# A gated linear unit on one core: three load slots and products in place, for two load slots and two output slots

## The chip, the cores and the metric

The kernel runs on one core of a Trainium2 chip. The metric is the time of one execution on the device in microseconds, taken as the median of several runs. Four engines of the core matter here: ACT (ScalarE) computes the sigmoid and issues the stores, DVE (VectorE) and POOL (GpSimd) multiply, SP (SyncE) issues the loads. The transfers themselves are done by 16 DMA engines that all queues of the core share.

## What is computed

```python
def setup_inputs():
    return {"x": np.random.randn(8192, 8192).astype(np.float32)}

def reference(x):
    a, b = np.split(x, 2, axis=-1)
    return a * (1 / (1 + np.exp(-b)))
```

Of each row of 8192 floats the first half, a, is multiplied by the sigmoid of the second half, b. 268.4 MB are read and 134.2 MB are written, each byte once.

## The kernel before

**Tiles.** The 8192 rows are cut into 32 tiles of 256 rows (line 20). A tile has two rows of x on each of the 128 partitions, so that a partition holds 64 KiB of input (row 0: a, b; row 1: a, b) and 32 KiB of output (line 21 and 22 lay out the two tensors accordingly; both sides of each transfer are contiguous on a partition). The output of a tile is again two rows, one behind the other.

**Slots.** There are two load slots of 64 KiB and two output slots of 32 KiB on each partition (lines 25 and 26). Tile i uses load slot i mod 2 and output slot i mod 2.

**Work on a tile** (`work`, lines 72 to 89). ACT replaces b by its sigmoid in the load slot (line 82). DVE or POOL multiplies a by it and writes the product to the output slot (line 84). A middle tile is worked on in two pieces, each over both rows: the first 768 columns (`cut`, line 30), whose product POOL makes from tile 2 on, and the other 3328, whose product DVE makes. The first and the last tile are worked on in four pieces, half a row each (`fourths`, line 32), by DVE alone.

**Transfers.** A load is one DMA of 8 MB issued by SP (line 63); the first tile's load is two DMAs, one for each row (line 37). A store is one DMA of 4 MB issued by ACT (line 68). The first tile is stored as two DMAs of 16 KiB on a partition, one for each row; the last one as one of 16 KiB and two of 8 KiB (line 39). For the last tile, `behind` is 1 (line 40), so that its first store stands behind the third sigmoid in ACT's order.

**Order and waits.** The waits are chosen by hand: `place` (line 48) declares for each instruction that it depends, within its slot, on nothing but the instructions handed to it, and keeps it in program order on its engine.

- Load i+2 waits for the products of tile i, which are the last readers of its slot (line 62). It does not wait for a store.
- The sigmoids of tile i wait for load i, and in the middle tiles for store i-2, which frees the output slot (lines 78 to 82). In the last tile the products wait for that store (line 88).
- A product waits for its sigmoid, a store for the products that it sends (line 69).

The loop (lines 93 to 103) issues, for each tile, its sigmoids and products, then load i+2 on SP, then the store on ACT. So the sigmoids of tile i+1 stand behind store i on ACT, which itself waits for the products of tile i.

Two functions rework the finished program and are the same before and after: `_launch_early` moves the first load to the front of SP's program, and `_close_on_sync` shortens the end, so that SP waits last for the last store.

Of the kernel before, what the change touches and what calls it, by code (L numbers as in the profile page):

```python
# [8 lines left out]
def _tiles(ctx, tc, x, out):  # L9
    nc = tc.nc  # L10
    P = nc.NUM_PARTITIONS
    DEP = mybir.DependencyInfo(mybir.DependencyClass.Sync, mybir.DependencyReason.DATA)
    fp32 = mybir.dt.float32
    SIG = mybir.ActivationFunctionType.Sigmoid

    n_rows, n_cols = x.shape
    half = n_cols // 2
    R = 2
    SLOTS = 2
    n_tiles = n_rows // (P * R)  # L20
    x_g = x.rearrange("(g p h r) m -> g h p (r m)", p=P, h=2, r=R)
    out_g = out.rearrange("(g p h r) m -> g h p (r m)", p=P, h=2, r=R)

    pool = ctx.enter_context(tc.tile_pool(name="io", bufs=1))
    xs = [pool.tile([P, R * n_cols], fp32, name=f"x_sb{k}") for k in range(SLOTS)]
    os = [pool.tile([P, R * half], fp32, name=f"o_sb{k}") for k in range(SLOTS)]

    whole = [(0, 8)]
    rows = [(0, 4), (4, 8)]
    cut = half // 16 * 3  # L30
    few_and_most = [(0, 8, 0, cut), (0, 8, cut, half)]
    fourths = [(k, k + 2, k % 4 * half // 4, (k % 4 + 2) * half // 4) for k in range(0, 8, 2)]
    loads = [whole] * n_tiles
    works = [few_and_most] * n_tiles
    stores = [whole] * n_tiles
    behind = [0] * n_tiles
    loads[0] = stores[0] = rows
    works[0] = works[-1] = fourths
    stores[-1] = [(0, 4), (4, 6), (6, 8)]
    behind[-1] = 1  # L40

    def meet(a, b):
        return a[0] < b[1] and b[0] < a[1]

    traced = [[] for _ in range(SLOTS)]
    load_of, mul_of, store_of = {}, {}, {}

    def place(i, ins, *needs):


        kept = {n.ins.name for n in needs}
        for e in traced[i % SLOTS]:
            if e.ins.name not in kept:
                tc.declare_no_dep(ins.ins, e.ins, reason="follows from the waits that are kept")
        traced[i % SLOTS].append(ins)
        tc.keep_in_program_order(ins)
        return ins

    def load(i):
        for lo, hi in loads[i]:  # L60
            c = slice(lo * n_cols // 4, hi * n_cols // 4)
            free = [m for w, m in mul_of.get(i - SLOTS, []) if meet(w, (lo, hi))]
            ins = nc.sync.dma_start(out=xs[i % SLOTS][:, c], in_=x_g[i // 2, i % 2, :, c])  # L63
            load_of.setdefault(i, []).append(((lo, hi), place(i, ins, *free)))

    def store(i, lo, hi):
        c = slice(lo * half // 4, hi * half // 4)
        ins = nc.scalar.dma_start(out=out_g[i // 2, i % 2, :, c], in_=os[i % SLOTS][:, c])  # L68
        done = [m for w, m in mul_of[i] if meet(w, (lo, hi))]
        store_of.setdefault(i, []).append(((lo, hi), place(i, ins, *done)))  # L70

    def work(i, lo, hi, near, far):

        rows = xs[i % SLOTS].rearrange("p (r h m) -> p r h m", r=R, h=2)
        packed = os[i % SLOTS].rearrange("p (r m) -> p r m", r=R)
        r, c = slice(lo // 4, (hi + 3) // 4), slice(near, far)
        b = rows[:, r, 1, c]
        landed = [s for w, s in load_of[i] if meet(w, (lo, hi))]
        gone = [s for w, s in store_of.get(i - SLOTS, []) if meet(w, (lo, hi))]
        by_sigmoid = 0 < i < n_tiles - 1  # L80
        needs = [*landed, *(gone if by_sigmoid else ())]
        sig = place(i, nc.scalar.activation(out=b, in_=b, func=SIG), *needs)  # L82
        engine = nc.gpsimd if far == cut and i > 1 else nc.vector
        mul = engine.tensor_mul(out=packed[:, r, c], in0=rows[:, r, 0, c], in1=b)  # L84
        if by_sigmoid:
            for s in gone:
                tc.add_manual_dep(sig.ins, s.ins.name, DEP, reason="frees the output slot")
        place(i, mul, sig, *(() if by_sigmoid else gone))
        mul_of.setdefault(i, []).append(((lo, hi), mul))

    for i in range(SLOTS):
        load(i)
    for i in range(n_tiles):
        due = list(stores[i])
        for k, piece in enumerate(works[i]):
            work(i, *piece)
            ready = works[i][k - behind[i]][1] if k >= behind[i] else 0
            while len(stores[i]) > 1 and k < len(works[i]) - 1 and due[0][1] <= ready:
                store(i, *due.pop(0))
        if i + SLOTS < n_tiles:  # L100
            load(i + SLOTS)
        for lo, hi in due:
            store(i, lo, hi)


def _launch_early(nc):
# [68 lines left out]
@with_exitstack  # L175
def kernel(
    ctx: ExitStack,
    tc: tile.TileContext,
    x: bass.AP,
    out: bass.AP,  # L180
):
    nc = tc.nc
    with ExitStack() as pools:
        _tiles(pools, tc, x, out)
    tc.close()
    tc.compile()
    _launch_early(nc)
    _close_on_sync(nc)
# [30 lines left out]
```

## Time and profile before

| | us |
|---|---|
| median of 3 runs (932.70 to 932.84) | 932.84 |
| the profiled execution, first to last instruction | 931.1 |
| ACT busy | 229.8 |
| DVE busy | 232.5 |
| POOL busy | 99.9 |
| a middle tile's sigmoids (two pieces) | 1.48 and 5.73 |
| its products (POOL, DVE) | 3.44 and 7.09 |
| a sigmoid of half a row, a product of half a row | 1.90, 2.29 |
| a 4 MB store, from issue to landing (median) | 43.6 |
| an 8 MB load, from issue to landing (median) | 43.5 |

The profiled execution has no total time beside its span. The medians of the runs lie 1.7 us above the span; they hold what lies around it.

How to read it: "q1" is the DMA queue of SP (the loads), "q10" that of ACT (the stores). A time from issue to landing holds the time that a transfer stands behind others, and the time in which it shares the DMA engines with the other queue. "ACTq" and "SPq" are the sequencers of ACT and SP, which issue DMAs and wait. A line of the timeline has the start, the time from the start of the first to the end of the last of the instructions merged in it, engine, operation and shape, and in brackets how long the engine stood idle before, and what ended that.

### The profile page before, as it was taken

Reading aid. Unit: us, or ns where it says so; the run is one execution under the profiler, and the core shown is the slowest. Engines: PE = TensorE matmul, PEld = TensorE weight load, DVE = VectorE, ACT = ScalarE, POOL = GpSimd, SP = SyncE. Lnnn points to the kernel's source line nnn. Section 1 sums busy time; section 2 is a strip of 40 time slices with the busy share of each in tenths; the row PEclk is TensorE's granted clock in tenths of the full one; section 3 lists DMA queues with packets and bytes.
Section 4 is the critical chain, followed back from the end, with each engine's and each line's share of the span. In section 5 each row is a group of like instructions: output and inputs, shape, how many; then the busy total and the mean of one; then the engine's idle time right before and its main releaser. Section 6 shows DMA issues by size and latency. Waiting matters only on the chain.

```text
span 931.1 us, 325 instructions
## 1 busy us (share of the span) xinstructions
DVE 232.5 (25%) x39; ACT 229.8 (25%) x69; POOL 99.9 (11%) x33
## 2 busy tenths in 40 slices
DVE  1133311333113331133320333203332033320233
ACT  2123332033320333203332023320233302333023
POOL 0001111011110111101111011110111101111010
DMA  9999999999999999999999999999999999999998
GB/s 405 450 439 417 428 450 424 455 405 428 450 428 450 407 469 409 428 450 427 452 405 450 428 428 450 424 452 408 428 450 428 450 408 465 411 428 450 427 452 383
DMA packets 9793, 402.67 MB, mean 432 GB/s; under 512 B 1088, under 2 KB 1088, under 8 KB 1088
## 3 DMA queue, kind: packets, MB, share of 16 engines
q1 hardware_dynamic: 4752, 268.44, 66.6%
q10 hardware_dynamic: 5040, 134.22, 33.4%
q14 instruction: 1, 0.01, 0.0%
HBM read 268.44 MB, written 134.22 MB: 432 GB/s over the span
## 4 chain that ended last, share of the span: by engine, by line
DMA 75%; DVE 12%; ACT 12%; issue 0%; ACTq 0%; SPq 0%
DMA out_dram<-o_sb 65%; DVE o_sb L84 12%; ACT x_sb L82 12%; DMA x_sb<-in_x_dram 10%; ACTq L68 0%; SPq L63 0%
## 5 line engine op out<-in xcount | busy, mean ns | idle before, releaser
L84 DVE TENSOR_TENSOR o_sb<-x_sb 128x6656 f32<-128x6656 f32 (+2 forms) x39 | 232.5, 5970 | 690.2 <-ACT x_sb L82 690.2
L82 ACT ACTIVATE x_sb<-x_sb 128x1536 f32<-128x1536 f32 (+1 forms) x68 | 228.5, 3407 | 689.9 <-DMA out_dram<-o_sb 630.0
L84 POOL TENSOR_TENSOR o_sb<-x_sb 128x1536 f32<-128x1536 f32 x29 | 99.7, 3437 | 787.7 <-ACT x_sb L82 787.7
L82 ACT ACT_TABLE_LOAD x1 | 1.3, 1283 | 0.8 <-PEq L203 0.8
L203 POOL MEMSET const-float32-0.0<- 128x1 f32 x1 | 0.1, 98 | 0.2 <-issue 0.2
L203 POOL MEMSET const-bfloat16-1.0<- 128x1 bf16 x1 | 0.1, 101 | 0.0
L203 POOL MEMSET const-uint8-127<- 128x1 uint8 x1 | 0.1, 101 | 0.0
L203 POOL MEMSET const-float32-1.0<- 128x1 f32 x1 | 0.1, 98 | 0.0
## 6 DMA issues: line engine op xcount, KB each, us to landing
out_dram<-o_sb ACTq DMA_DIRECT2D x30, 4096.0 KB, 43.6
x_sb<-in_x_dram SPq DMA_DIRECT2D x2, 4096.0 KB, 16.4
out_dram<-o_sb ACTq DMA_DIRECT2D x3, 2048.0 KB, 28.0
out_dram<-o_sb ACTq DMA_DIRECT2D x2, 1024.0 KB, 8.3
x_sb<-in_x_dram SPq DMA_DIRECT2D x31, 43.5
```

The source lines that it names most:

```text
L82: sig = place(i, nc.scalar.activation(out=b, in_=b, func=SIG), *needs)
L84: mul = engine.tensor_mul(out=packed[:, r, c], in0=rows[:, r, 0, c], in1=b)
L203: nc = _bacc.Bacc("TRN2", target_bir_lowering=False, num_devices=1)
```

## The change

- Three load slots of 64 KiB, no output slots. Together they take the same 192 KiB of a partition.
- Products overwrite the slot's row 0: the product of row 0 goes where a of row 0 was, the product of row 1 where b of row 0 was (`product`). So the 32 KiB of output lie together at the slot's start and are stored from there.
- Three loads are issued ahead of the loop (the first still as two DMAs). Load i+3 waits for the landing of store i, where load i+2 waited for the products of tile i.
- Sigmoids (`gate`) wait for their load alone.
- In the first and the last tile each product also waits for the products before it in the tile, since row 1's products overwrite what row 0's have read.
- The first tile is stored as 8 KiB (after its first product, with the store ahead of the second sigmoid on ACT) and 24 KiB (after its last), where it was 16 and 16. The last tile is stored as before: 16, 8 and 8 KiB, the first behind the third sigmoid.
- In the loop load i+3 comes behind store i in the program, each on its own engine.

```diff
-    SLOTS = 2
+    SLOTS = 3
...
-    os = [pool.tile([P, R * half], fp32, name=f"o_sb{k}") for k in range(SLOTS)]
...
+    few = half // 16 * 3
+    by_fourths = [(r, h * half // 2, (h + 1) * half // 2) for r in (0, 1) for h in (0, 1)]
...
     def load(i):
-        for lo, hi in loads[i]:
-            c = slice(lo * n_cols // 4, hi * n_cols // 4)
-            free = [m for w, m in mul_of.get(i - SLOTS, []) if meet(w, (lo, hi))]
+        for r in (0, 1) if i == 0 else (None,):
+            c = slice(None) if r is None else slice(r * n_cols, (r + 1) * n_cols)
             ins = nc.sync.dma_start(out=xs[i % SLOTS][:, c], in_=x_g[i // 2, i % 2, :, c])
-            load_of.setdefault(i, []).append(((lo, hi), place(i, ins, *free)))
...
+            load_of.setdefault(i, []).append(place(i, ins, *store_of.get(i - SLOTS, [])))
+
+    def store(i, lo, hi, *done):
+        ins = nc.scalar.dma_start(out=out_g[i // 2, i % 2, :, lo:hi], in_=xs[i % SLOTS][:, lo:hi])
+        store_of.setdefault(i, []).append(place(i, ins, *done))
+
+    def gate(i, rows, c):
+        b = xs[i % SLOTS].rearrange("p (r h m) -> p r h m", r=R, h=2)[:, rows, 1, c]
+        landed = load_of[i] if len(load_of[i]) == 1 else [load_of[i][rows.start]]
+        return place(i, nc.scalar.activation(out=b, in_=b, func=SIG), *landed)
+
+    def product(i, engine, r, c, *needs):
+
+        v = xs[i % SLOTS].rearrange("p (r h m) -> p r h m", r=R, h=2)
+        ins = engine.tensor_mul(out=v[:, 0, r, c], in0=v[:, r, 0, c], in1=v[:, r, 1, c])
+        return place(i, ins, *needs)
+
+    def ends(i, stores):
+        done = []
+        for k, (r, lo, hi) in enumerate(by_fourths):
+            c = slice(lo, hi)
+            done.append(product(i, nc.vector, slice(r, r + 1), c, gate(i, slice(r, r + 1), c), *done))
+            for a, z, after, at in stores:
+                if at == k:
+                    store(i, a, z, *done[: after + 1])
+
+    def middle(i):
+        done = []
+        for engine, c in ((nc.gpsimd if i > 1 else nc.vector, slice(0, few)), (nc.vector, slice(few, half))):
+            sig = gate(i, slice(0, 2), c)
+            done.append(product(i, engine, slice(0, 2), c, sig))
+        store(i, 0, R * half, *done)
+
+    q = half // 2
     for i in range(SLOTS):
         load(i)
     for i in range(n_tiles):
...
+        if i == 0:
+            ends(i, [(0, q, 0, 0), (q, 4 * q, 3, 3)])
+        elif i == n_tiles - 1:
+            ends(i, [(0, 2 * q, 1, 2), (2 * q, 3 * q, 2, 3), (3 * q, 4 * q, 3, 3)])
+        else:
+            middle(i)
         if i + SLOTS < n_tiles:
             load(i + SLOTS)
-        for lo, hi in due:
-            store(i, lo, hi)
```

More of the change, by code (lines that the diff above doesn't have):

```diff
@@ L11, in _tiles @@
     P = nc.NUM_PARTITIONS
-    DEP = mybir.DependencyInfo(mybir.DependencyClass.Sync, mybir.DependencyReason.DATA)
     fp32 = mybir.dt.float32
@@ L25, in _tiles @@
     xs = [pool.tile([P, R * n_cols], fp32, name=f"x_sb{k}") for k in range(SLOTS)]
-    os = [pool.tile([P, R * half], fp32, name=f"o_sb{k}") for k in range(SLOTS)]
[L28 to L43, printed above, removed]
+    few = half // 16 * 3
+    by_fourths = [(r, h * half // 2, (h + 1) * half // 2) for r in (0, 1) for h in (0, 1)]
     traced = [[] for _ in range(SLOTS)]
@@ L59, in load @@
     def load(i):
-        for lo, hi in loads[i]:
-            c = slice(lo * n_cols // 4, hi * n_cols // 4)
-            free = [m for w, m in mul_of.get(i - SLOTS, []) if meet(w, (lo, hi))]
+        for r in (0, 1) if i == 0 else (None,):
+            c = slice(None) if r is None else slice(r * n_cols, (r + 1) * n_cols)
             ins = nc.sync.dma_start(out=xs[i % SLOTS][:, c], in_=x_g[i // 2, i % 2, :, c])
-            load_of.setdefault(i, []).append(((lo, hi), place(i, ins, *free)))
[L66 to L89, printed above, removed]
+            load_of.setdefault(i, []).append(place(i, ins, *store_of.get(i - SLOTS, [])))
@@ L93, in _tiles @@
     for i in range(n_tiles):
[L94 to L99, printed above, removed]
+        if i == 0:
[4 more added lines that the diff above has]
+            middle(i)
         if i + SLOTS < n_tiles:
             load(i + SLOTS)
-        for lo, hi in due:
-            store(i, lo, hi)
 def _launch_early(nc):
```

## The prediction

> **What bounds the kernel now.** I read the page first, then a table of stretches, the two tables of waits (engines, then SP's queue), the timeline at both ends, and last the packet records of the trace, where each DMA engine's descriptors stand with start, length and bytes. The page:
>
> ```profile
> span 931.1 us, 325 instructions
> DMA  9999999999999999999999999999999999999998
> q1 hardware_dynamic: 4752, 268.44, 66.6%
> q10 hardware_dynamic: 5040, 134.22, 33.4%
> HBM read 268.44 MB, written 134.22 MB: 432 GB/s over the span
> ```
>
> No slice of the DMA row is empty, and the two queues' shares add up to 100% of 16 engines. The stretches (columns: stretch, length, DVE, ACT and POOL busy, clock, DMA share, GB/s) say that the rate is the same for loads alone (11 to 21), for the mixture and for stores alone (912 to 920, 438; packets are counted whole, so short stretches swing):
>
> ```profile
> 11.00:21.00 10.00, 4.49 (x2) 3.71 (x2) 0.00 (x0) 1.00 1.01 433
> 46.00:910.00 864.00, 214.53 (x31) 213.67 (x60) 99.67 (x29) 1.00 1.00 433
> 912.00:920.00 8.00, 6.40 (x3) 6.65 (x4) 0.00 (x0) 1.00 1.01 438
> ```
>
> The records agree: a 64 KiB load packet takes 2.418 us, a 32 KiB store packet 1.213, a 16 KiB one 0.611, an 8 KiB one 0.309, in every part of the run. All data packets added up and divided by 16 engines are 930.8 us, of a span of 931.1. Empty are only the first 1.01 us, before the first load packet, and about 0.3 at the end. The waits look worse than they are:
>
> ```profile
> ACT x_sb L82 <- DMA out_dram<-o_sb: 630.0, 29, 22.1
> ```
> ```profile
> SPq L63 <- DVE o_sb L84: 855.5, 30, 32.1
> ```
>
> ACT waits 630 us for stores and SP 855 us for products, but the transfers behind those waits are in a line that never runs dry. The chain of waits agrees: 75% of the span is DMA, and the 12% each of ACT and DVE on it are periods in which the engines moved other tiles.
>
> So the kernel is bound by bytes through 16 engines. The change moves the same bytes, in the same 264 load packets and 280 store packets for each engine (the packet counts above, less 16 completion records for each of 33 and 35 DMAs, over 16). It can gain under 1 us. It can lose wherever both queues are empty at once.
>
> **The order of packets.** In the records load and store packets alternate one to one on each engine once both queues hold work, whatever their size: a round is 2.42 + 1.21 = 3.63 us, a tile 8 rounds, 29.0 us. Call the lead the number of load packets that start before the first store packet. It is 17 now (the first store packet starts at 23.58, after the first packet of tile 1's load). When the last load packet ends, 264 - 17 = 247 store packets are done; tile 30's store ends with packet 256, so 9 are left, 10.9 us. The records: loads end at 910.10, that store at 921.00. This backlog is what covers the last tile's computing:
>
> ```profile
> 911.66 5.51 ACT L82 ACTIVATE x_sb<-x_sb 128x2048 f32<-128x2048 f32 x3 [21.67 <-DMA x_sb<-in_x_dram]
> 918.13 0.34 ACTq L68 DMA_DIRECT2D out_dram<-o_sb  x1
> 918.51 1.91 ACT L82 ACTIVATE x_sb<-x_sb 128x2048 f32<-128x2048 f32 x1 [1.35 <-DVE o_sb L84]
> 920.33 2.79 ACTq L68 DMA_DIRECT2D out_dram<-o_sb  x2
> ```
>
> From the last load packet's end to the start of its first sigmoid 1.56 us, from there to the issue of the first store 6.47, then d us from issue to first packet: 8.03 + d must be covered, and 10.9 does it. Its first packet starts at 920.42, straight behind tile 30's last on the same engine, so d is at most 2.29.
>
> **The change, part by part.**
>
> *Products in place* (39 products; DVE 7.09 us, POOL 3.44, the fourths 2.29; no operation is added or taken away). The trace shows no product in place, but the sigmoid is in place, 0.86 ns for an element (5.73 us / 6656) against the product's 1.07. Bounds for DVE are that rate and POOL's 2.24: -1.4 to +7.8 us in a middle tile, -0.9 to +4.8 on the last tile's first two products. From load to store a middle tile needs 1.48 + 5.73 + 7.09 = 14.35 us with the gaps, and below I find 7 us to spare. Taken: 0, by the sigmoid, which shows no price of being in place. In the last tile products now wait for their predecessor on DVE too, where two took 4.49 us; the gap that the trace shows at such hand-overs between ACT and DVE is 0.02 us. Taken: 0.
>
> *The first tile's store as 8 and 24 KiB.*
>
> ```profile
> 11.98 3.71 ACT L82 ACTIVATE x_sb<-x_sb 128x2048 f32<-128x2048 f32 x2 [9.91 <-DMA x_sb<-in_x_dram]
> 13.92 4.49 DVE L84 TENSOR_TENSOR o_sb<-x_sb 128x2048 f32<-128x2048 f32 x2 [13.92 <-ACT x_sb L82]
> 18.45 0.37 ACTq L68 DMA_DIRECT2D out_dram<-o_sb  x1
> 21.68 3.71 ACT L82 ACTIVATE x_sb<-x_sb 128x2048 f32<-128x2048 f32 x2 [5.99 <-DMA x_sb<-in_x_dram]
> ```
>
> The small store goes out after one product: 13.92 + 2.29 = 16.2, 2.2 us earlier. ACT then stands until 16.2 with the second sigmoid behind it, which ends near 18.5 instead of 15.7; the third starts only when the second half has landed, at 21.68, so that is hidden. Without this cover it would cost 2.7 us of tile 0, which no transfer waits for at that time. Packets: 8 x 0.309 + 8 x 0.91 (24 KiB by size) = 9.75 us against 16 x 0.611 = 9.78: 0. What counts is the lead. The store issued at 18.45 missed the packet start at 20.84 and took the next, at 23.26: its delay x under load is 2.39 to 4.81. From 16.2 it is ready at 18.6 to 21.0, and takes the start at 19.6 (lead 15, x below 3.4), at 20.8 (lead 16) or at 23.3 (lead 17, x over 4.6).
>
> *A third load at the start, and load i+3 behind store i.* The wait for products goes, a wait for the landing of a store comes on SP; behind it on SP stand only later loads. Which wait ends last there? With lead n, store i ends n - 16 packets after the end of load i+2. With lead 15 two load packets are still queued behind store i's end, so load i+3 has 7.25 us. It needs 0.37 to 0.53 (a store's last packet to its landing, in the records), 0.02 for the wait, and from issue to first packet 1.01 (the first load, idle engines) to 4.81: 1.4 to 5.4. It is in time. With lead 16 it has 3.63, so from x above 3.1 it comes late, a store packet takes its turn, and the lead becomes 15. Lead 17 can't last: the load would be wanted before the store is done. Even in a gap of the load queue the engines work on stores, so this costs no time here; the backlog pays.
>
> By the Trainium skill (DMA: Bandwidth & Descriptors, "Anatomy of one DMA") a completion waits until the last byte is confirmed in the target memory, which is most of a fixed 2 us and longest for HBM. It speaks against making a load wait for a store. The trace has 0.53 us; by the page's figure the load with lead 15 would come after at most 6.9 us, still in time, and the sum would stay.
>
> *The output slots' wait goes from ACT.* Sigmoid i no longer waits for store i-2, which landed 0.17 us after the load it needs (99.63 against 99.46): 0.17 us, on a tile with 7 us to spare. Store i+1 is issued 1.6 + 14.4 + d = 17 to 18 us after load i+1's end; with lead 15 its turn comes after 7 rounds, 25.4. If that were gone, loads would run on at the same rate.
>
> *The last tile* keeps its order on ACT: three sigmoids, the 2 MB store, a sigmoid, two stores of 1 MB. Its cover falls to 15 - 8 = 7 packets, 8.49 us, against 8.03 + d: the engines stand idle for d - 0.46. For d the nearest row is the first load on idle engines, 1.01 to 1.35 by engine; 2.29 is the ceiling. I take 1.35, as the slowest engine ends last: 0.9 us. Restarting idle engines costs 0 (first store packets, 0.611 like all) to 0.81 (first load packets, up to 2.02 against 1.21); taken 0.3, nearer to the stores. By the Trainium skill (the same page, "Latency and other measured facts") the first byte of such a DMA comes after some 600 ns; with 0.34 of issue the sum would be 0.5 + 0.3. No run here has a store on idle engines.
>
> **Sum.** 0 + 0 + 0 + 0.9 + 0.3 = +1.2 on the profiled 931.1: 932.3. The median shown, 932.84, lies 1.7 above that span, so the time is **934.0 us**, +0.13%. A measurement of this kernel can tell some 0.2%, 1.87 us, from no change. Own bounds: d 1.01, no restart, +0.55; d 2.29 and 0.81, +2.65: 933.4 to 935.5.
>
> **The rivals.**
>
> *Hidden anyway* (15 in 100): the lead stays 16. Eight packets cover 9.70, the gap is d - 1.67, at most 0.6 and likely none: +0 to +0.6, about 933.0. For it: lead 16 needs only 3.63 us of answer, and an idle load queue may answer in 1.5. Against it: x was at least 2.39.
>
> *Slower: the load queue runs dry early* (20 in 100). If x is over 4.6, the first store again comes after 17 loads, load 3 finds its slot still being stored, and several store packets run together; or an answer takes longer than 7.25 us later on. The lead falls to 14 or 13. It can't fall lower: tile 30's store is ready 1.6 + 14.4 + 1.35 = 17.3 us, five rounds, after load 30's end, so at least 5 packets are left. With 14, 6 packets cover 7.28, the gap is d + 0.75 = 2.1, with the restart +2.4: 935.2. With 13, +3.6: 936.4. Against it: stores are issued 2.2 us earlier. For it: x isn't known above 2.39.
>
> *Faster* (3 in 100): only the 1.3 us of empty ends could shrink, so 932 at best, unless packets get shorter; no stretch shows one shorter than its bytes.
>
> *The products in place take longer, or a two-row product on POOL waits for DVE* (2 in 100): a middle tile can hide 7 us, the last tile pays; 20% on its first two products is +0.9 more, 934.9, POOL's rate +4.8.
>
> **Chances.** The forecast has 60. Of it a sixth has d and restart over 2.33 together, which is past +1.87. Slower by over 0.2%: 20 + 10 + 1 = 31, faster 3, within 66. The range, 932.7 to 935.9, takes in the hidden case, the forecast's bounds and the rival with lead 14, and leaves out lead 13 and a gain.
>
> **What would show it.** The middle should keep 29.0 us for a tile and 433 GB/s; SP should wait for stores, and ACT for loads alone. The first store should be issued at 16.2, the last load land near 914 (two store packets later than 911.6), the last tile's first store go out near 920.6, with an empty 1 us of DMA after tile 30's store ends near 921. It is wrong if the middle's period changes, if DMA idles anywhere ahead of 900, or if the last load lands as before.

## The result, and the profile after

| | before | after |
|---|---|---|
| median, us (20 runs each) | 932.66 | 933.98 |
| lowest to highest, us | 932.45 to 932.85 | 933.79 to 934.38 |
| span of the profiled execution, us | 931.1 | 932.8 |

The ratio after to before is 1.0014, its 95% interval 1.0008 to 1.0020: the changed kernel is slower by 1.3 us, against 934.0 us forecast. The sum came out; two of its terms did not, as shown below.

The page of the changed kernel, its span and its DMA row:

```profile
span 932.8 us, 298 instructions
DMA  9999999999999999999999999999999999999998
```

Its stretches (columns: stretch, length, DVE, ACT and POOL busy, clock, DMA share, GB/s):

```profile
46.00:910.00 864.00, 214.53 (x31) 213.67 (x60) 99.67 (x29) 1.00 1.00 434
921.88:922.29 0.41, 0.41 (x1) 0.41 (x1) 0.00 (x0) 1.00 0.00 0
```

The middle is as before: the same rate within 1 GB/s, the same busy times, a tile every 29.0 us. What is new stands in the second line: 0.41 us in which no DMA engine moves anything. The two tables of waits (engines, then SP's queue) show that the waits changed hands as the diff says, for no time:

```profile
ACT x_sb L55 <- DMA x_sb<-in_x_dram: 689.0, 33, 22.6
```
```profile
SPq L45 <- DMA out_dram<-x_sb: 867.3, 29, 66.4
```

Of all transfers ACT now waits for loads alone, SP for stores. The timeline at both ends (start, time, engine, operation, idle before):

```profile
12.10 1.91 ACT L55 ACTIVATE x_sb<-x_sb 128x2048 f32<-128x2048 f32 x1 [10.04 <-DMA x_sb<-in_x_dram]
14.04 2.29 DVE L60 TENSOR_TENSOR x_sb<-x_sb 128x2048 f32<-128x2048 f32 x1 [14.04 <-ACT x_sb L55]
16.36 0.38 ACTq L49 DMA_DIRECT2D out_dram<-x_sb  x1
16.79 1.91 ACT L55 ACTIVATE x_sb<-x_sb 128x2048 f32<-128x2048 f32 x1 [2.78 <-DVE x_sb L60]
...
914.99 5.51 ACT L55 ACTIVATE x_sb<-x_sb 128x2048 f32<-128x2048 f32 x3 [21.88 <-DMA x_sb<-in_x_dram]
916.94 6.70 DVE L60 TENSOR_TENSOR x_sb<-x_sb 128x2048 f32<-128x2048 f32 x3 [16.70 <-ACT x_sb L55]
921.46 0.34 ACTq L49 DMA_DIRECT2D out_dram<-x_sb  x1
```

The first store is issued at 16.36, behind one product, 2.1 us earlier than before. The last load is there for its sigmoid at 914.99, 3.3 us later than before, and the last tile's first store follows 6.47 us behind it, as before. In the packet records tile 30's store ends between 920.89 and 921.87, engine by engine, and the next store packet starts at 922.30 to 922.45 on all of them. Before, the one followed the other without a gap.

The records of the same execution, put in order for each engine as their ends and starts meet (L a load packet, s a store packet, from the first one on; most of the engines of a row follow it):

```
before, all 16 engines   17 L, then sLsLsLsL...        9 s after the last L
after, 11 engines        15 L, then sLssLsL...         7 s after the last L
after, 5 engines         16 L, then ssLsLsL...         8 s after the last L
```

One more thing changed there. Some load packets are longer than their bytes (1.213 us for 32 KiB, 2.418 for 64 KiB). One engine of each kernel, around its first store packet, as kind, KiB, start and length:

```
before  L32 19.93 1.21   L64 21.14 2.48   s16 23.62 0.61   L64 24.23 2.42
after   L32 17.46 1.21   L32 18.67 1.59   s8  20.26 0.31   L32 20.56 1.21
```

The load packet ahead of the first store packet is stretched (on the five engines with 16 loads the one ahead of that), as if the engine stood while it took up the other queue; the records show no more than that the packet is longer. Added up from 12 to 70 us and divided by 16 engines, such time beyond the bytes (the excess from here on) is 0.34 us before and 0.97 after. Of the 0.97, 0.55 lie at 38 to 42 us, where the 8 KiB pieces end and the 24 KiB ones begin.

So there are two candidates: 0.6 us of stretched packets at the start, and idle DMA engines at the end.

### The profile page after: what moved, and what is told of

Same layout as the page of the kernel before. It is cut to its first block, busy times and chain, and to the rows that moved or that the text cites. A ratio compares the mean times of both kernels' runs of the same rounds, so it can differ in the third digit from the quotient of the medians.

```text
span 932.8 us, 298 instructions
## 1 busy us (share of the span) xinstructions
DVE 232.6 (25%) x39; ACT 229.9 (25%) x69; POOL 99.9 (11%) x33
## 5 line engine op out<-in xcount | busy, mean ns | idle before, releaser
L60 DVE TENSOR_TENSOR x_sb<-x_sb 128x6656 f32<-128x6656 f32 (+2 forms) x39 | 232.6, 5970 | 693.5 <-ACT x_sb L55 693.5
L60 POOL TENSOR_TENSOR x_sb<-x_sb 128x1536 f32<-128x1536 f32 x29 | 99.7, 3437 | 790.9 <-ACT x_sb L55 790.9
```

The source lines that it names most:

```text
L60: ins = engine.tensor_mul(out=v[:, 0, r, c], in0=v[:, r, 0, c], in1=v[:, r, 1, c])
```

## The experiments

The theory was the prediction's: time is lost where both queues are empty, and what decides is how many store packets are left when the loads end (the backlog). The main rival: the new ring of slots costs time by itself, through the loads' wait for a store's landing or the products in place. All times are medians; the kernel before, beside them, ran at 932.63 to 932.68.

**1. The kernel before, with the new first store.** Two load slots, output slots and the old waits stay.

```diff
-    loads[0] = stores[0] = rows
+    loads[0] = rows
+    stores[0] = [(0, 2), (2, 8)]
```

> The kernel before with one edit: the first tile is stored as 8 and 24 KiB, the first piece right behind its first product. Theory (backlog of stores at the end): the first store packet starts after 15 or 16 load packets in place of 17, 7 or 8 store packets in place of 9 are left of tile 30 when the loads end, the last tile's computing is no longer covered, and the time is some 1.3 us over the kernel before, about 934.0, although this kernel has two load slots, output slots and no wait for a landing. Rival (the loads' wait for a store's landing, or the products in place, cost the time): no difference from the kernel before, 932.7.

Measured: 933.95 us, ratio 1.0015 (1.0006 to 1.0023). The packets lie as in the changed kernel (lead 15 or 16, 7 or 8 left), the excess from 12 to 70 us is 1.00, and the end has the same hole (stretches: the middle, and the time in which all engines are idle):

```profile
46.00:910.00 864.00, 214.53 (x31) 213.67 (x60) 99.63 (x29) 1.00 1.00 434
921.74:921.90 0.16, 0.16 (x1) 0.16 (x1) 0.00 (x0) 1.00 0.00 0
```

The whole loss is here without a third slot, without the wait for a landing, without products in place. For this loss the rival is not needed.

**2. The changed kernel, with the old first store.**

```diff
-            ends(i, [(0, q, 0, 0), (q, 4 * q, 3, 3)])
+            ends(i, [(0, 2 * q, 1, 1), (2 * q, 4 * q, 3, 3)])
```

> The changed kernel with the first tile stored as 16 and 16 KiB behind its second and fourth product, as the kernel before has it. Theory (backlog, which the wait for the landing caps): the first store packet comes after 17 loads again, but load 3 then finds its slot still being stored, store packets run without loads between them, and the backlog falls back to 6 to 8 packets: 934.0 to 935.2. Rival (the small first store alone costs the time): 932.7, as before.

Measured: 935.67 us (935.07 to 936.29), ratio 1.0033 (1.0021 to 1.0044): more than the upper end expected, on the theory's side. 17 loads come first; load 3 is issued at 70.72, when the last packet of load 2 has already ended (69.5), and each engine moves five or six store packets in a row. After that 6 are left at the end. The issue of load 3, and the stretch in which all engines stand still:

```profile
70.72 0.33 SPq L45 DMA_DIRECT2D x_sb<-in_x_dram  x1
...
921.46:923.19 1.73, 1.73 (x2) 0.45 (x1) 0.00 (x0) 1.00 0.00 0
```

So the ring costs little in the middle (0.36 us of excess between 70 and 110 us, after the load queue has run dry), but it caps the backlog, and the early small store is what keeps its load queue from running dry. What the loss is charged to therefore depends on the order: in the kernel before, the small first store costs 1.3 us and the ring adds nothing to it; once the ring is there, the same store saves 1.7 us (935.67 to 933.98). Why the median is 0.6 us above the profiled execution's 935.07 the one profile can't say.

**3. The changed kernel, with the last tile stored in four pieces.** This closes the hole and touches nothing else.

```diff
-            ends(i, [(0, 2 * q, 1, 2), (2 * q, 3 * q, 2, 3), (3 * q, 4 * q, 3, 3)])
+            ends(i, [(0, q, 0, 1), (q, 2 * q, 1, 2), (2 * q, 3 * q, 2, 3), (3 * q, 4 * q, 3, 3)])
```

> The changed kernel with the last tile stored in four pieces of 8 KiB, each as soon as its product is there, the first behind the second sigmoid. Theory: the first store of the last tile is issued some 4.3 us after its first sigmoid starts in place of 6.5, which is 6.8 us after the last load packet against 8.5 us of store packets left, so nothing is idle any more: 932.6 to 932.9, equal to the kernel before, with three slots, the wait for the landing and the products in place all kept. Rival (slots, wait or products in place cost it in the middle): stays at 934.0.

Measured: 933.38 us, ratio 1.0008 (0.9999 to 1.0017). Its timeline at the end:

```profile
914.75 3.71 ACT L55 ACTIVATE x_sb<-x_sb 128x2048 f32<-128x2048 f32 x2 [21.86 <-DMA x_sb<-in_x_dram]
916.69 4.49 DVE L60 TENSOR_TENSOR x_sb<-x_sb 128x2048 f32<-128x2048 f32 x2 [16.68 <-ACT x_sb L55]
919.01 0.34 ACTq L49 DMA_DIRECT2D out_dram<-x_sb  x1
```

The store is issued 4.26 us after the sigmoid starts, and no engine has a gap any more. 0.60 us came back, about half of the loss; 0.7 us stayed, more than expected. The excess from 12 to 70 us is 1.01. That the stretched packets are this rest was the next theory.

**4. The kernel before, with the first tile stored whole.**

```diff
-    loads[0] = stores[0] = rows
+    loads[0] = rows
```

> The kernel before with the first tile stored in one piece after its fourth product. Theory: the first store packet comes after 21 or 22 loads, but tile 0 has 8 store packets for each engine in place of 16, so only 5 or 6 packets are left at the end of the loads, 6.1 to 7.3 us against 9.0 needed: idle for 1.7 to 2.9, time 934.4 to 935.6. Rival (only the wait for the landing can cost): 932.7.

Measured: 935.15 us, ratio 1.0026 (1.0016 to 1.0036), within the range expected, though not only by the idle time that the theory has. 6 or 7 packets are left where 5 or 6 were expected, and the last line of its stretches is empty again; the load packets ahead of the first store packet take 3.3 to 3.6 us in place of 2.42, 0.99 us on average, which the theory did not have.

```profile
921.59:923.30 1.71, 1.71 (x2) 0.45 (x1) 0.00 (x0) 1.00 0.00 0
```

**5. The kernel before, with the last tile in four pieces** (a control: `stores[-1] = [(0, 2), (2, 4), (4, 6), (6, 8)]`).

> The kernel before with the last tile stored in four pieces of 8 KiB, the first behind the second sigmoid. Control. Theory: nothing was idle at this kernel's end, so there is nothing to gain: 932.6 to 932.8. Rival (four small stores are faster by themselves, and that is what brought the changed kernel from 933.98 to 933.38): about 932.1.

Measured: 932.70 us, ratio 0.9999 (0.9990 to 1.0008). Four pieces gain nothing where nothing was idle. The excess of its profiled execution is 0.66 us, against 0.34 in the kernel before with the same start: executions differ by that much.

**6. The kernel before, with the new first store and the last tile in four pieces** (the edits of 1 and 5 together).

> The kernel before with the first tile stored as 8 and 24 KiB and the last one in four pieces. Theory now (two terms: 0.6 to 0.7 us in which the engines wait for the early store's packets near 18 and 40 us, which shows as lengthened load packets, and about as much idle before the last tile's first store): the second term goes, the first stays, without three slots or the wait for a landing: 933.2 to 933.5. Rival (what was left in the changed kernel with four last stores belongs to its three slots): 932.7.

Measured: 933.44 us, ratio 1.0007 (0.9998 to 1.0016). No engine is idle at the end, the excess from 12 to 70 us is 0.94. This is experiment 3 without its three slots, and the same rest of 0.76 us. Each of the two intervals alone reaches down to no change. But all 11 runs here (from 933.06) lie above 26 of the 27 of the kernel before beside them (up to 932.87), and the records account for the rest: in the four kernels with no idle time at the end (before, experiments 3, 5 and 6) the span less the excess is 930.8, 930.8, 930.8 and 930.9 us. So what stayed is the excess at the start; why those packets are longer is not shown.

**7. The changed kernel, with the old first store and the last tile in four pieces** (the edits of 2 and 3).

> The changed kernel with the first tile stored as 16 and 16 KiB and the last one in four pieces. Theory: 5 or 6 store packets are left (6.1 to 7.3 us) against 6.8 needed, so 0 to 0.7 us idle, and 0.4 us in which load packets are lengthened when the load queue has run dry near 75: 933.0 to 934.0, against 935.67 without the four last stores. Rival (the 3 us of that kernel come from the middle): stays near 935.5.

Measured: 934.08 us, ratio 1.0018 (1.0008 to 1.0028), from 933.28 to 937.16; the median lies 0.1 us above the range expected. The 1.6 us against experiment 2 come from the edit at the end alone. The runs spread more than those of any other kernel but one; the profiled one, at 933.29, has 0 to 0.5 us idle at the end, so what the longer ones lose was not seen.

**8. The kernel before, with the first tile in pieces of 8, 8 and 16 KiB, none of them early.** This was to tell early stores from small ones.

```diff
-    loads[0] = stores[0] = rows
+    loads[0] = rows
+    stores[0] = [(2, 4), (0, 2), (4, 8)]
```

> The kernel before with the first tile stored as three pieces of 8, 8 and 16 KiB, the first (the second half of row 0) issued behind the second product, at 18.5 as in the kernel before, so 17 loads come first again. What costs the 0.6 to 0.7 us at the start, the early arrival or the small pieces? If the early arrival of the first store: 932.6 to 932.8. If the 8 KiB pieces and the passage to the next store: 933.1 to 933.4. The backlog at the end is larger than before (17 packets), so nothing is idle there by either.

Measured: 941.0 us, ratio 1.0086 (1.0073 to 1.0100), which neither side had put. The execution that was profiled took 956.71 us, so another was taken:

> The kernel with the first tile stored in three pieces of 8, 8 and 16 KiB once more, for an undisturbed profile. With 24 store packets for tile 0 in place of 16 its store should land so late that tile 2's sigmoids, which wait for it in this kernel, hold up store 2 and load 4, until both queues are empty for some 6 us near 99 us; from there on no more idle time, and about 941 in all. Rival: the idle time comes from pieces of 8 KiB being slow, and is spread over the first 100 us.

This one took 959.84 us, not 941, so it shows the hole and not the whole time; the other has the same hole, from 99.2 to 105.5 us. Two lines of its stretches and two of its timeline:

```profile
98.90:105.00 6.10, 5.77 (x1) 0.00 (x0) 0.00 (x0) 1.00 0.00 0
...
500.00:750.00 250.00, 58.40 (x9) 56.98 (x16) 27.50 (x8) 1.00 1.00 418
```
```profile
90.42 7.12 ACT L83 ACTIVATE x_sb<-x_sb 128x1536 f32<-128x1536 f32 x2 [39.53 <-DMA out_dram<-o_sb]
...
104.76 0.35 ACTq L69 DMA_DIRECT2D out_dram<-o_sb  x1
```

Here the backlog is too long. Tile 0's store has 24 packets, each behind a load packet of 64 KiB, and lands at 90; tile 2's sigmoids need its output slot and wait 39.5 us; load 4 and store 2 can only be issued 14.3 us after them. By 98.9 both queues are empty, and all engines stand for 6.1 us. The hole explains most of the 8.3 us. Past 500 us this execution's load packets are longer than their bytes (418 GB/s where 434 is usual); that cause is open. So is the question that the kernel was made for, with one hint: up to 40 us, where it moves 8 KiB pieces that start at 23.3 behind 64 KiB loads, the excess is 0.05 and 0.08 us in the two executions, and 0.27 and 0.28 come near 64.8, in the load packets ahead of the first 16 KiB piece.

**9. The changed kernel, with the last tile stored whole** (`ends(i, [(0, 4 * q, 3, 3)])`), a known delay put on the step in question.

> The changed kernel with the last tile stored whole behind its fourth product: its store is issued 11.15 us after the first sigmoid starts in place of 6.49, 4.66 later. Theory (nothing covers the last tile's computing beyond the 7 or 8 packets): every us of it shows, 933.98 + 4.7 = 938.6. Rival (something else delays the end): under 937.

Measured: 938.12 us, ratio 1.0059 (1.0042 to 1.0076), 4.1 us more than the changed kernel for 4.4 us by which its store is issued later behind the sigmoid (its timeline, then its stretch without any transfer):

```profile
914.85 7.31 ACT L55 ACTIVATE x_sb<-x_sb 128x2048 f32<-128x2048 f32 x4 [21.73 <-DMA x_sb<-in_x_dram]
916.79 8.90 DVE L60 TENSOR_TENSOR x_sb<-x_sb 128x2048 f32<-128x2048 f32 x4 [16.54 <-ACT x_sb L55]
925.72 0.34 ACTq L49 DMA_DIRECT2D out_dram<-x_sb  x1
```
```profile
921.80:926.50 4.70, 3.89 (x2) 0.36 (x1) 0.00 (x0) 1.00 0.00 0
```

What comes late at the end shows nearly in full.

No version here is faster than the kernel before; the best of the others (experiment 5) equals it.

## Why the prediction was right, and where it was not

- **Bound by bytes, nothing to gain.** Right: 433 or 434 GB/s and 29.0 us a tile in every kernel but that of experiment 8. (The packets' 930.8 us and the 1.3 us of empty ends add up to more than the span of 931.1, because the records of one engine overlap, by some 2.2 us in all.)
- **Products in place: 0.** Right. The four shapes take 7.09, 3.44, 2.29 and 1.76 us as before, and the last tile's first three products 6.70 against 6.69.
- **The wait for a store's landing: 0, by the lead of 15.** Right in its result, by other numbers than the step's. From the start on no engine of the changed kernel moves more than two store packets in a row, and two only at the end of a load, where the load queue's turn goes to its 4-byte completion record. So load i+3 is always there for its turn. But a store's landing was put at 0.37 to 0.53 us behind its last packet, and it takes 2.72 to 2.81 for every store that a load waits for. In the records one load packet (2.42 us) stands between a store's last packet and its completion record, on every engine; before there was none, and the landing took 0.5 to 0.65. The engines are also 2.8 us apart. For the first such load, the first engine ends the store at 62.96 and the last at 65.81, it lands at 68.57, the load is issued at 68.65, and its first packet starts at 72.78: 9.8 us, where the step needed at most 5.4 and had 7.25. No turn was lost, because the load queue's completion record and two store packets went between the last packet of its earlier load (70.36 on that engine) and 72.78. How much was to spare is not shown: from issue to first packet it took 4.1 us, and about as long in experiment 2, where the load queue stood empty (70.72 to 74.79). The 2 us that the prediction quotes from the Trainium skill (DMA: Bandwidth & Descriptors, "Anatomy of one DMA") stand there for DMAs issued from GpSimd. The stores here are issued from ACT, and the 2.7 us are mostly the load packet in between. Experiment 2 shows the other branch of that step (lead 17 can't last) and its price, 3.0 us, where the rival that ends with 6 packets put 2.4.
- **The first tile's store: "What counts is the lead."** Half right. The lead fell to 15 on eleven engines and 16 on five, where the step had one lead for all, for a store issued at 16.36 against 16.2 forecast. But the step's own time was put at 0, on packet lengths alone, and it costs some 0.7 us (experiments 3 and 6: 0.74 and 0.76 over the kernel before once the end is covered). The term left out is the stretched load packets where the store queue starts and where it passes to the next store.
- **The last tile: 0.9 idle + 0.3 restart.** Right in its mechanism (experiments 1, 3 and 9), too large in size: closing the hole gives back 0.60 us in the changed kernel and 0.51 in the kernel before (933.95 to 933.44). Issue to first packet, d, is 0.84 to 0.99 in the changed kernel, where 1.35 was taken, and the same within 0.01 in experiments 1, 2, 4 and 9. By engine the idle time is 0.43 to 1.56 us; on the engine whose load ends last, at 913.40, it is 8.03 + d less 8.49, or 0.4, with the numbers of the step. The first packet of the last tile's store takes 0.612 to 0.622 us, so a restart stretches it by 0.01 at most, and all packets from there on by 0.17 for an engine, which experiment 3 does not show. 0.43 and 0.17 make the 0.60 that came back. By the Trainium skill (DMA: Bandwidth & Descriptors, "Latency and other measured facts") the first byte of such a DMA comes after some 600 ns. With the 0.34 us of issue that is an estimate of 0.94 us, and the 0.84 to 0.99 here agree with it better than with the row that was preferred.
- **The sum.** 1.2 was forecast as 0 + 1.2, and 1.3 is some 0.7 + 0.6. The two errors cancelled, which is luck; the forecast was nearer than its terms deserved. The time itself, 934.0 against 933.98, comes nearer still by its base: 932.84, from three runs, lies 0.18 above the median of 20. The 1.7 us between that median and the span compare two executions; a run's time lies 1.4 us above its own span (934.2 against 932.8).
- **What would show it.** The last load's landing was put near 914 and came at 914.97; of the 3.3 us of lateness two store packets are 2.4, and the stretched packets most of the rest. The last tile's first store went out at 921.46, where 920.6 was put, and all engines were empty together for 0.41 us, where an empty 1 us was put.

## What to carry to other kernels

When the transfers never pause, ask first where both queues can be empty together: count the packets left in the store queue when the last load ends, and hold their time against the last tile's way from landing to first store packet. That backlog is set at the very start, by how many loads come ahead of the first store and in how many pieces it goes, and here it stayed for the whole run; too short leaves the end uncovered, and too long runs into whatever waits for a store's landing. A control that makes the same edit in the other kernel, as in experiment 1, separates a ring of buffers from the small edit that came with it. And when a forecast comes out, hold each of its terms against the trace: here one was too small, one too large, and a landing that cost nothing took some five times what it was given.

## What the runs showed of the hardware

- Load and store packets of 64 and 32 KiB alternated one to one on each engine over 900 us, so the lead of 15 to 17 packets was still there at the end.
- A store's 4-byte completion record takes a turn like any packet. Where it came directly behind the store's last packet, the store landed 0.5 to 0.65 us after that packet (the kernel before, while loads ran); where a load packet went first, 2.7 to 2.8 us (the changed kernel; in experiment 1, while loads ran, 3.05 for the first store and 2.72 to 2.84 for the others).
- Where the store queue started, load packets of 32 KiB were stretched by 0.06 to 0.51 us (0.38 on average) after the change. Behind load packets of 64 KiB the average was 0.02 us or less for a first store packet of 8 KiB (experiment 8), 0.21 to 0.37 for one of 16 KiB (the kernel before, experiments 2, 5 and 7) and 0.99 for one of 32 KiB (experiment 4). The passage to the 24 KiB pieces cost an engine 0.4 to 0.8 us more, that from 24 to 32 KiB nothing. What sets the length is open.
- With a store that came at 16.4 us, between load packets of 32 KiB, the engines no longer took it up after the same packet: five after 16, eleven after 15. From there they ran up to 2.8 us apart (the first tile's second store ends at 62.96 on the first engine and at 65.81 on the last), against 0.5 before, and the last tile had to wait for the slowest (its load ends between 911.36 and 913.40).
